# RMSNorm and matrix product on one core: the last four output tiles stored one by one, the very last in two pieces of 68 and 60 rows

## The chip, the cores and the metric

The kernel runs on one core of one Trainium2 chip. The time is the device time of one execution in microseconds (us). A core has engines that run side by side: TensorE (PE, with its weight loads shown apart as PEld), VectorE (DVE), ScalarE (ACT), GpSimd (POOL), and SyncE (SP), which here does nothing but issue DMA transfers and wait. Sixteen DMA engines carry the transfers between the chip's memory (HBM) and the core's own memory.

## The reference

```python
def reference(x, gamma, weight, eps):
    rms = np.sqrt(np.mean(x ** 2, axis=-1, keepdims=True) + eps)
    x_norm = x / rms * gamma
    return np.matmul(x_norm, weight).astype(np.float32)
```

x has 16 x 1024 = 16,384 rows of 512 numbers, weight is 512 x 768, and the output has 16,384 rows of 768 numbers, all float32. So 33.6 MB of x and 1.6 MB of weights are read, and 50.3 MB are written.

## The kernel before, in words

The rows are cut into 128 tiles of 128 rows. Each tile is brought in, cast to bfloat16 on GpSimd, turned by TensorE (four 128-column blocks, taken two at a time as 32-bit words), multiplied with the weights (already multiplied by gamma), and the product is scaled with the row's factor 1/rms on its way out of the accumulator: ScalarE does this for even tiles, VectorE for odd ones. The factor comes from squares summed on ScalarE.

Tiles are held in groups of eight: one output buffer `ot` holds 128 partitions x 8 tiles x 768 numbers, and there are three such buffers. In a group, partition p holds eight consecutive rows of the output, so that tile t of the group is row t of each partition's eight. A store of n tiles therefore writes, per partition, one run of n x 3,072 bytes; runs of neighbouring partitions lie eight rows apart.

`stretches` (line 46) says in which pieces a group is loaded or stored: as a rule all eight tiles at once (3 MB per store), in smaller pieces at the start, and at the end. Line 57 sets the pieces of the stores: 4 and 4 tiles in the last group but one (tiles 112 to 119), and 2, 2, 2, 1, 1 in the last (tiles 120 to 127). `store` (line 149) is called after every tile and issues a DMA from SP when the tile is the last of its piece.

All loads and stores are issued by SP in the order of the program. The order is written out by hand (`manual_schedule`). SP waits for the engines that filled the buffer, and for the DMA that used the same one of eight completion semaphores before. After the last store it waits for all transfers to land, and the kernel ends.

The last two tiles (lines 288 to 294) are finished differently: each in two parts of 512 and 256 columns, each part with its own accumulator, the first scaled by ScalarE and the second by VectorE; then the tile is stored.

Of the kernel before, what the change touches and what calls it, by code (L numbers as in the profile page):

```python
# [18 lines left out]
def kernel(  # L19
# [8 lines left out]
    nc = tc.nc  # L28
    P = 128

    x = x.flatten_outer_dims()
    out = out.flatten_outer_dims()
# [3 lines left out]
    NT = N // P  # L36
    NP = NT // 2
    G = 8
    NG = NT // G
# [6 lines left out]
    def stretches(parts):  # L46
        first, size, i = {}, {}, 0
        for g in range(NG):
            for n in parts.get(g, [G]):
                for t in range(i, i + n):  # L50
                    first[t], size[t] = i, n
                i += n
        return first, size

    opening = [1, 2, 1, 2, 2]
    x_first, x_size = stretches({0: opening, 1: [4, 4]})
    o_first, o_size = stretches({0: opening, NG - 2: [4, 4], NG - 1: [2, 2, 2, 1, 1]})

    def rows(ap, i, n):
        if i < G:  # L60
            return ap[i * P:(i + n) * P, :].rearrange("(p t) d -> p t d", t=n)
        return ap.rearrange("(g p t) d -> g p t d", p=P, t=G)[i // G, :, i % G:i % G + n, :]
# [11 lines left out]
    x_tiles, xb_tiles, tp_tiles, rstd_of, xT_tiles, o_tiles = {}, {}, {}, {}, {}, {}  # L74

    def held(tiles, i, n=1):
        return tiles[i // G][:, i % G:i % G + n, :]
# [66 lines left out]
    def out_tile(i):  # L144
        if i // G not in o_tiles:
            o_tiles[i // G] = outp.tile([P, G, O], F32, name="ot")
        return o_tiles[i // G][:, i % G, :]

    def store(i):
        first, n = o_first[i], o_size[i]  # L150
        if i == first + n - 1:
            nc.sync.dma_start(out=rows(out, first, n), in_=held(o_tiles, first, n))

    def matmul(i, k, acc, lo, hi):
        nc.tensor.matmul(out=acc[:, lo:hi], lhsT=xT_tiles[i // 2][:, i % 2, k // 2, :, k % 2], rhs=w_bf[:, k, lo:hi],  # L155
# [10 lines left out]
    def finish_tile(i, acc, engine):  # L166
        scale(engine, out_tile(i), acc[:, :O], rstd_of[i])
        store(i)
# [16 lines left out]
    with tc.manual_schedule():  # L185
# [102 lines left out]
        for i in (NT - 2, NT - 1):  # L288
            for lo, hi, engine in ((0, WIDE, nc.scalar), (WIDE, O, nc.vector)):
                a = accumulator()  # L290
                for k in range(K):
                    matmul(i, k, a, lo, hi)
                scale(engine, out_tile(i)[:, lo:hi], a[:, lo:hi], rstd_of[i])
            store(i)
# [35 lines left out]
```

## Time and profile before

| what | us |
|---|---|
| median of 9 runs | 211.26 |
| lowest and highest of them | 210.8, 212.88 |
| the profiled execution, its own time | 211.27 |
| its span (first to last instruction) | 209.5 |
| TensorE busy | 198.4 |
| ScalarE busy | 158.2 |
| VectorE busy | 111.7 |
| GpSimd busy | 66.3 |

In the profile, a busy row is a string of digits, one for each fortieth of the span (5.2 us): 9 means busy for 90% or more. The DMA row is the mean busy share of the sixteen DMA engines, and GB/s is what they moved. In a table of stretches each row has the window, its length, the busy time and number of instructions of PE, PEld, DVE, ACT and POOL, and then the granted TensorE clock, the DMA share and GB/s. A row of waits names who waited, at which line, for whom: total us, number, longest.

The stores as the page lists them, with size and median time from issue to landing:

```profile
out_dram<-ot SPq DMA_DIRECT2D x13, 3072.0 KB, 20.3
...
out_dram<-ot SPq DMA_DIRECT2D x6, 768.0 KB, 7.3
out_dram<-ot SPq DMA_DIRECT2D x2, 1536.0 KB, 9.3
...
out_dram<-ot SPq DMA_DIRECT2D x4, 384.0 KB, 18.0
```

The four stores of 384 KB are two at the start of the kernel and the two of tiles 126 and 127. At the end of the kernel SP issues stores at these times, in us from the start of the span: tiles 120-121 at 195.26, 122-123 at 198.68, 124-125 at 200.73, tile 126 at 201.49, tile 127 at 202.79.

### The profile page before, as it was taken

How to read it: one execution, taken by the hardware profiler on the slowest of the kernel's cores; microseconds unless marked ns; L12 is line 12 of the kernel's file. 1: busy time of each engine (PE TensorE's matmuls, PEld its weight loads, DVE VectorE, ACT ScalarE, POOL GpSimd, SP SyncE). 2: the span in 40 equal slices, each digit the busy share in tenths (PEclk: the TensorE clock that was granted, in tenths of full speed). 3: DMA queues.
4: the chain of work that ended last, by engine and by line, in shares of the span. 5: the costliest groups of instructions: out<-in, count | busy, mean ns of one | idle time of the engine just before them, and what ended most of it. 6: DMA issues, size and time to landing. Idle time of an engine off the chain costs nothing.

```text
span 209.5 us, 3555 instructions
## 1 busy us (share of the span) xinstructions
PE 198.4 (95%) x1268; PEld 137.5 (66%) x1293; DVE 111.7 (53%) x204; ACT 158.2 (76%) x388; POOL 66.3 (32%) x71
## 2 busy tenths in 40 slices
PE   7799999999999999999999999999999999999960
PEld 3466766677666676667766667666776666766630
DVE  2565565466456545644654565456446545654630
ACT  4699778778777877887787778778877877787830
POOL 1256543233323323332332233233323323310000
PEclk9999999999999999999999999999999999999996
DMA  6999999999999999999999999999999999998992
GB/s 225 410 426 441 382 403 427 419 443 424 443 419 418 447 418 433 422 421 444 416 444 416 443 424 427 436 415 438 421 433 419 436 432 430 422 415 369 381 369 110
DMA packets 7206, 85.69 MB, mean 409 GB/s; under 512 B 1042, under 2 KB 1044, under 8 KB 3220
## 3 DMA queue, kind: packets, MB, share of 16 engines
q1 hardware_dynamic: 6912, 85.46, 96.8%
q8 instruction: 10, 0.16, 0.3%
q10 hardware_dynamic: 276, 0.00, 0.1%
q14 instruction: 8, 0.07, 0.1%
HBM read 35.13 MB, written 50.33 MB: 408 GB/s over the span
## 4 chain that ended last, share of the span: by engine, by line
PE 93%; DVE 2%; issue 1%; ACT 1%
PE ops L155 78%; PE tp L120 13%; PE ops L210 1%; DVE ot L139 1%; DVE xT L127 1%; ACT ot L137 0%; DVE xb L93 0%; ACT jk L97 0%; DVE w_bf L139 0%; PE tp L224 0%; ACT rms L101 0%; DVE warm L201 0%; DVE rstd L103 0%; DVE eps_sb L203 0%
## 5 line engine op out<-in xcount | busy, mean ns | idle before, releaser
L155 PE MATMUL ops<-w_bf,xT 128*128 128x512 bf16 (+1 forms) x999 | 192.5, 324 | 1.9 <-DVE w_bf L139 0.6
L155 PEld LDWEIGHTS <-xT 128*128 128x128 bf16 x1024 | 100.2, 98 | 57.0 <-issue 1.0
L93 POOL CAST xb<-xt 128x1024 bf16<-128x1024 f32 (+1 forms) x65 | 65.6, 1014 | 118.7 <-PE tp L120 103.8
L127 DVE COPY xT<-tp 128x1024 bf16<-128x1024 bf16 (+1 forms) x67 | 44.5, 666 | 80.9 <-PE tp L120 80.9
L137 ACT ACTIVATE ot<-ops,rstd 128x768 f32<-128x768 f32 (+1 forms) x65 | 58.1, 894 | 37.8 <-PE ops L155 36.9
L97 ACT ACTIVATE jk<-xt 128x512 bf16<-128x512 f32 x128 | 78.7, 619 | 1.3 <-DMA xt<-in_x_dram 1.3
L120 PE MATMUL tp<-ident_f,xb 128*128 128x128 f32 x256 | 69.0, 274 | 0.7 <-DVE xb L93 0.6
L139 DVE TENSOR_SCALAR ot<-ops,rstd 128x768 f32<-128x768 f32 (+1 forms) x65 | 64.5, 992 | 2.9 <-PE ops L155 2.8
L120 PEld LDWEIGHTS tp<-ident_f,xb 128*128 128x128 f32 x256 | 35.9, 141 | 4.1 <-issue 1.1
L97 ACT ACTIVATION_READ_ACCUMULATOR jk<-xt 128x1 f32 x128 | 24.4, 191 | 0.0
L101 ACT ACTIVATE rms<-ssq,eps_sb 128x2 f32<-128x2 f32 (+1 forms) x64 | 18.9, 296 | 2.0
L103 DVE RECIPROCAL rstd<-rms 128x2 f32<-128x2 f32 (+1 forms) x64 | 9.9, 155 | 3.2 <-ACT rms L101 3.1
L210 PE MATMUL ops<-warm 128*128 128x512 bf16 x11 | 4.2, 523 | 1.2 <-DVE eps_sb L203 1.2
L210 PEld LDWEIGHTS <-warm 128*128 128x128 bf16 x11 | 1.3, 129 | 2.5 <-DVE eps_sb L203 1.2
L137 ACT ACTIVATE w_bf<-w_f,g_sb 128x768 bf16<-128x768 f32 x2 | 1.9, 936 | 1.4 <-DMA w_f<-in_weight_dram 1.4
L192 ACT ACT_TABLE_LOAD x1 | 1.3, 1283 | 1.7 <-issue 1.7
L93 DVE CAST xb<-xt 128x512 bf16<-128x512 f32 x2 | 1.2, 592 | 2.4 <-DMA xt<-in_x_dram 2.4
L139 DVE TENSOR_SCALAR w_bf<-w_f,g_sb 128x512 bf16<-128x512 f32 (+2 forms) x3 | 1.4, 481 | 0.5 <-DMA w_f<-in_weight_dram 0.5
L224 PEld LDWEIGHTS tp<-ident_f,g_row 2*128 2x128 f32 x2 | 0.3, 201 | 0.8 <-issue 0.8
L201 DVE MEMSET warm<- 128x256 uint32 x1 | 0.3, 272 | 0.9 <-PEq L311 0.9
L224 PE MATMUL tp<-ident_f,g_row 2*128 2x2 f32 x2 | 0.4, 265 | 0.0
L226 DVE COPY g_sb<-tp 128x4 f32<-128x4 f32 x1 | 0.2, 163 | 0.4 <-PE tp L224 0.4
(7 smaller groups left out, 1.0 us busy)
## 6 DMA issues: line engine op xcount, KB each, us to landing
out_dram<-ot SPq DMA_DIRECT2D x13, 3072.0 KB, 20.3
xt<-in_x_dram SPq DMA_DIRECT2D x14, 2048.0 KB, 24.8
out_dram<-ot SPq DMA_DIRECT2D x6, 768.0 KB, 7.3
out_dram<-ot SPq DMA_DIRECT2D x2, 1536.0 KB, 9.3
xt<-in_x_dram SPq DMA_DIRECT2D x2, 1024.0 KB, 11.2
xt<-in_x_dram SPq DMA_DIRECT2D x3, 512.0 KB, 5.8
w_f<-in_weight_dram SPq DMA_DIRECT2D x2, 768.0 KB, 6.1
out_dram<-ot SPq DMA_DIRECT2D x4, 384.0 KB, 18.0
```

The source lines that it names most:

```text
L93: engine.tensor_copy(out=xb_tiles[i // 2][:, i % 2:i % 2 + n, :], in_=held(x_tiles, i, n))
L97: nc.scalar.activation(out=jk, in_=held(x_tiles, i)[:, 0, :], func=AF.Square, accum_out=ssq)
L101: nc.scalar.activation(out=rms[:, :n], in_=ssq[:, :n], func=AF.Sqrt, scale=1.0 / D, bias=eps_sb)
L103: nc.vector.reciprocal(out=rstd[:, :n], in_=rms[:, :n])
L120: nc.tensor.transpose(out=tp_tiles[j][:, t, h, :], in_=words[:, lo:lo + P], identity=ident_f)
L127: nc.vector.tensor_copy(out=dst[:, t:t + n, :], in_=src[:, t:t + n, :])
L137: nc.scalar.mul(out=dst, in_=src, mul=r)
L139: nc.vector.tensor_single_scalar(out=dst, in_=src, scalar=r, op=mybir.AluOpType.mult)
L155: nc.tensor.matmul(out=acc[:, lo:hi], lhsT=xT_tiles[i // 2][:, i % 2, k // 2, :, k % 2], rhs=w_bf[:, k, lo:hi], start=(k == 0), stop=(k == ...
L192: nc.scalar.preload_act_table(AF.Sqrt)
L210: nc.tensor.matmul(out=spare[:, :WIDE], lhsT=warm[:, :P], rhs=warm, start=True, stop=True)
L224: nc.tensor.transpose(out=gp[:, c, :], in_=g_row[:, :, c], identity=ident_f[:2, :2])
```

## The change

The last group is stored in pieces of 2, 2, 1, 1, 1 and 1 tiles, so tiles 124 and 125 go apart. The store of tile 127 is issued as two DMAs: first its partitions 60 to 127 (68 rows), then its partitions 0 to 59 (60 rows). Nothing that is computed changes. On SP's queue there are two more DMAs; the instructions of the other engines stay in the same order.

```diff
-    o_first, o_size = stretches({0: opening, NG - 2: [4, 4], NG - 1: [2, 2, 2, 1, 1]})
+    o_first, o_size = stretches({0: opening, NG - 2: [4, 4], NG - 1: [2, 2, 1, 1, 1, 1]})
...
     def store(i):
         first, n = o_first[i], o_size[i]
         if i == first + n - 1:
-            nc.sync.dma_start(out=rows(out, first, n), in_=held(o_tiles, first, n))
+            for lo, hi in ((60, P), (0, 60)) if i == NT - 1 else ((0, P),):
+                nc.sync.dma_start(out=rows(out, first, n)[lo:hi], in_=held(o_tiles, first, n)[lo:hi])
```

## The prediction, before the changed kernel was run

> **What bounds the kernel now.** I read the page first, then what SP (the engine that issues the DMAs) waits for, then the stretches of the last 20 us, then the trace's records of single DMA packets and of the semaphore steps at their landing.
>
> ```profile
> span 209.5 us, 3555 instructions
> PE 198.4 (95%) x1268; PEld 137.5 (66%) x1293; DVE 111.7 (53%) x204; ACT 158.2 (76%) x388; POOL 66.3 (32%) x71
> ...
> DMA  6999999999999999999999999999999999998992
> GB/s 225 410 426 441 382 403 427 419 443 424 443 419 418 447 418 433 422 421 444 416 444 416 443 424 427 436 415 438 421 433 419 436 432 430 422 415 369 381 369 110
> ```
>
> Two resources are full up to slice 39: TensorE and the sixteen DMA engines. The chain of waits gives TensorE 93%, but the change touches no matmul; what it touches begins where TensorE stops.
>
> ```profile
> 201.80 0.69 ACT L137 ACTIVATE ot<-ops,rstd 128x512 f32<-128x512 f32 x1 [0.61 <-PE ops L155]
> 201.82 0.38 PE L155 MATMUL ops<-w_bf,xT 128*128 128x256 bf16 x2
> 202.24 0.48 DVE L139 TENSOR_SCALAR ot<-ops,rstd 128x256 f32<-128x256 f32 x1 [0.82 <-PE ops L155]
> 202.79 0.33 SPq L152 DMA_DIRECT2D out_dram<-ot  x1
> ```
>
> The last arithmetic ends at 202.72 and the last store is issued at 202.79. The span ends 6.7 us later.
>
> ```profile
> SPq L325 <- DMA out_dram<-ot: 5.3, 1, 5.3
> ```
>
> SP's last real wait is 5.3 us for stores to land (203.23 to 208.54); 0.9 us of closing instructions follow. So what sets the end is the last DMA landing. How full are the engines in that wait?
>
> ```profile
> 190.00:195.00 5.00, 5.00 (x36) 3.52 (x34) 3.12 (x5) 4.28 (x12) 0.00 (x0) 1.00 0.86 360
> 195.00:199.00 4.00, 3.95 (x26) 2.53 (x25) 1.95 (x5) 3.08 (x7) 0.00 (x0) 1.00 0.92 381
> 199.00:202.00 3.00, 3.00 (x20) 1.76 (x18) 1.50 (x2) 1.12 (x3) 0.00 (x0) 1.00 0.84 345
> 202.00:204.00 2.00, 0.20 (x2) 0.00 (x0) 0.48 (x1) 0.49 (x1) 0.00 (x0) 1.00 0.99 399
> 204.00:205.00 1.00, 0.00 (x0) 0.00 (x0) 0.00 (x0) 0.00 (x0) 0.00 (x0) 1.00 1.01 409
> 205.00:206.00 1.00, 0.00 (x0) 0.00 (x0) 0.00 (x0) 0.00 (x0) 0.00 (x0) 1.00 0.53 206
> 206.00:207.00 1.00, 0.00 (x0) 0.00 (x0) 0.00 (x0) 0.00 (x0) 0.00 (x0) 0.60 0.09 37
> 207.00:208.50 1.50, 0.00 (x0) 0.00 (x0) 0.00 (x0) 0.00 (x0) 0.00 (x0) 0.50 0.04 16
> ```
>
> The DMA share (last column but one) is the finding. All sixteen are busy to 205; then it falls to 0.09 (about 1.5 engines of 16), then 0.04 over 1.5 us, which is one engine for 1 us. **One engine ends the kernel alone.** The landing records say by how much: each store raises its semaphore once per engine. Times in us:
>
> | store | most engines (median) | second last | last |
> |---|---|---|---|
> | tiles 122-123 | 201.84 | 203.15 | 204.78 |
> | tiles 124-125 | 203.92 | 205.01 | 206.63 |
> | tile 126 | 204.87 | 205.92 | 207.56 |
> | tile 127 | 205.87 | 206.86 | 208.48 |
>
> Following packets that abut, the last engine has no gap from 193 us on and lies 2.6 us behind the others; a second lies 1.0 behind. The last one's backlog is old: in the 3 MB stores its packets of 24,576 bytes take 941 to 964 ns where other engines take 912. In this tail its 3,072-byte packets start every 0.118 us as the others' do. Eight of them, its eight rows of tile 127, are the step from 207.56 to 208.48.
>
> **The change part by part.**
>
> *Tiles 124 and 125 stored apart.* One DMA of 6,144-byte packets becomes two of 3,072. Removed: nothing from the total of bytes. Added: one issue of 0.33 us on SP and one 4-byte semaphore packet of 9 ns per engine. Tile 124 is ready at 199.24 (ScalarE's 198.34 + 0.90), so it is issued at about 199.3 while SP would otherwise sleep until 200.73; tile 125 keeps its issue time. Gain on the ordinary engines: they finish 122-123 at 201.44 and start 124-125 at 201.59, so at most 0.15 us of idle. Gain on the last engine: **nothing**, it has no gap to fill; it pays the 9 ns.
>
> *Tile 127 as 68 and 60 rows.* Which engine gets which row decides everything. The packet records carry no engine number. The Trainium skill, "DMA: Bandwidth & Descriptors", section "Why a DMA increments its semaphore by 16 and not by 1", says that such a DMA uses the largest number up to 16 that divides its outer size, and the lowest-numbered engines. This trace agrees as far as it goes (the two-row gamma load made exactly two 1,024-byte packets). By it, 68 rows go as 17 each to engines 0 to 3 and 60 rows as 4 each to 0 to 14. So engines 0-3 have 21 rows instead of 8, engines 4-14 have 4, engine 15 has none. With 0.118 us per row, from the landing of tile 126:
>
> - ordinary engine among 0-3: 204.87 - 0.15 + 21 x 0.118 = 207.20
> - second-last engine among 4-14: 205.92 + 0.47 = 206.39
> - last engine, if it is 15: 207.56, done with tile 126
>
> The end moves from 208.48 to 207.56: **-0.92 us**. Only 0.36 us lower lies the load on engines 0-3, so nothing more is to be had. That those four run alone costs no speed, I take it: the one engine alone at the end kept 0.118 (bounds: 0 to +0.4 us, a fifth on 2 us, of which 0.36 is hidden).
>
> *SP's queue.* The second half is issued 0.38 us after the first (0.33 and its step), at 203.17; nothing is behind it but the closing waits. Its semaphore and the first half's are reused ones whose earlier stores landed by 192.75 and 196.57, so no new wait. From issue to first packet on an idle engine took 0.86 us (200.73 to 201.59), so the second half can start at 204.0, before engines 4-14 have finished tile 126. Hidden. If the closing waits see it land last instead, one more step of 0.06.
>
> *A rule that speaks against it.* The row first: in the tail, on an engine with a backlog, the last data packet of tile 126, its 9 ns semaphore packet and the first packet of tile 127 follow without a gap, and landing trails the last packet by about 0.4 us, beside the next packets. The same page ("Rules for kernel authors") says not to split a transfer into partition halves, since they serialize, and ("Anatomy of one DMA") gives each DMA some 2.0 us fixed plus bytes at 436 GB/s. By that, the pieces of 209 and 184 KB cost 2.48 + 2.42 = 4.9 us in turn against 2.9 whole: +2.0 us, 213.3. By the rows a further DMA in a full queue costs 0.01 us. I take the rows: the page's fixed part is mostly the wait for the receipt, which overlaps here.
>
> **Sum.** Span 209.48 - 0.92 = 208.56. The profiled execution took 211.27 (1.79 outside the span), so 210.35; the median before, 211.26, is the same within 0.01. I say **210.3 us**, -0.45%. A measurement of this kernel tells about 0.5% (1.06 us, to 210.2 or 212.3) from no change, so this is just inside "same".
>
> **Rivals.** All hang on which engine is last, and the trace can't number it.
>
> 1. *The last engine is one of 4-14.* It keeps 4 rows: 207.56 + 0.47 = 208.03, -0.45: **210.8**. For: the same page ("Latency and other measured facts") calls engines 7 and 15 usually the slower ones, and this trace does show exactly one with slow packets. Against: 15 is the other candidate, and the page blames a cause of DMAs issued from GpSimd, which this kernel has none of.
> 2. *The second-last engine is one of 0-3.* It would have 205.92 + 2.48 = 208.40, -0.08: **211.2**, nothing gained. For: it lags 1.0 us, enough to fill the slack; instruction fetches of 16 KB that take about 1 us each fall on single engines, so it can be any. Against: 4 of 15 by chance.
> 3. *The last engine is one of 0-3.* Then it gets 13 rows more: 207.56 + 21 x 0.118 = 210.04, +1.56: **212.8**, slower. It decides as soon as an engine of 0-3 lands tile 126 after 206.0 (208.48 - 2.48). For: nothing in the records excludes it, and 4 of 16 by chance. Against: the pace of this engine is its own, all through the run, and the page names two engines outside 0-3.
> 4. *The rows don't split as stated* (68 rows on sixteen engines, say): nothing moves, 211.2.
>
> **Numbers.** The forecast 0.58; rival 1 0.14; 2 0.13; 3 with the fixed-cost case 0.11; 4 0.04. Around the forecast I allow 0.35 us each way: the slow pace may add 0.05 to the eight rows, engines 0-3 may lose up to 0.4, the median of a set of runs moves by 0.2. Range 209.9 to 211.5 holds the forecast, 1, 2 and 4, and leaves rival 3 out. Faster by over 0.5%: half of the forecast's share (its centre is 0.15 from the bound) and a little of rival 1, 0.33. Slower 0.12. Within 0.5%: 0.55.
>
> **What would show it.** The DMA share of the last 1.5 us before the end: about four engines (0.25) and not one. SP's wait for the stores shorter by the 0.38 of the extra issue and by 0.92. Tile 124's issue near 199.3. In the landings: the 68-row store steps its semaphore by data four times, near 206.7; the last landing of all belongs to tile 126 at 207.56. Wrong if the last landing is a 68-row one after 208, or if the last engine still carries rows of tile 127.

## The result: slower by about one microsecond

The changed kernel took 212.14 us (median of 16 runs, 211.69 to 214.68); the kernel before, run beside it, 211.15 us (53 runs). The ratio is 1.0056, with a 95% interval of 1.004 to 1.0072. The forecast was 210.3 us, with a range of 209.9 to 211.5.

The profiled execution of the changed kernel took 213.24 us, 1.1 more than its median, so two differences have to be kept apart. First the head of the page, then the row of the costliest group in the page before and after: TensorE's matmuls, with busy time and mean ns, and after the second bar the idle time before them and what ended it. (Line 155 of the kernel before is line 158 of the changed one.)

```profile
span 211.5 us, 3558 instructions
PE 198.4 (94%) x1268; PEld 137.4 (65%) x1293; DVE 111.6 (53%) x204; ACT 158.2 (75%) x388; POOL 66.3 (31%) x71
```

```profile
L155 PE MATMUL ops<-w_bf,xT 128*128 128x512 bf16 (+1 forms) x999 | 192.5, 324 | 1.9 <-DVE w_bf L139 0.6
```

```profile
L158 PE MATMUL ops<-w_bf,xT 128*128 128x512 bf16 (+1 forms) x999 | 192.5, 324 | 3.3 <-DVE w_bf L139 2.0
```

In this execution the weights came later at the very start (TensorE waited 2.0 us for them and not 0.6), and all that follows is 1.2 us later: the last arithmetic ends at 203.92 (before: 202.72). The change touches nothing there, and the first experiment's kernel, which lacks the half of the change that costs, shows such a start too (1.7 us). What the change does is seen from 203.92 on. The stretches of the changed kernel, with the DMA share in the last column but one:

```profile
204.00:205.00 1.00, 0.00 (x0) 0.00 (x0) 0.00 (x0) 0.00 (x0) 0.00 (x0) 1.00 1.01 399
205.00:206.00 1.00, 0.00 (x0) 0.00 (x0) 0.00 (x0) 0.00 (x0) 0.00 (x0) 1.00 0.98 326
206.00:207.00 1.00, 0.00 (x0) 0.00 (x0) 0.00 (x0) 0.00 (x0) 0.00 (x0) 0.57 0.65 123
207.00:208.00 1.00, 0.00 (x0) 0.00 (x0) 0.00 (x0) 0.00 (x0) 0.00 (x0) 0.50 0.25 61
208.00:209.00 1.00, 0.00 (x0) 0.00 (x0) 0.00 (x0) 0.00 (x0) 0.00 (x0) 0.50 0.24 92
209.00:210.00 1.00, 0.00 (x0) 0.00 (x0) 0.00 (x0) 0.00 (x0) 0.00 (x0) 0.50 0.12 49
```

Where the kernel before had one engine at work for the last two microseconds (share 0.04 to 0.09), there are now four (0.25). And they are slow: at 207 to 208 a share of 0.25 moves 61 GB/s, at 208 to 209 nearly the same share moves 92. Before, all sixteen moved 409 at a share of 1.01, which is 102 for a quarter. So the four engines are busy, but their packets take longer. The packet records say the same: of the 512 packets of 3,072 bytes of the last four tiles, 39 take over 0.18 us (up to 0.94), between 205.48 and 208.03. The longest such packet in the tail of the kernel before takes 0.136. Below, "slow packets" are those over 0.18 us, and their excess is the time that each takes over 0.121 us, summed; in the changed kernel it is 9.3 us.

The landings (us; each store raises its semaphore once per engine):

| store, changed kernel | most engines (median) | last |
|---|---|---|
| tile 125 | 205.01 | 206.37 |
| tile 126 | 206.02 | 207.31 |
| tile 127, 68 rows, four engines | 209.14, 209.29, 209.30 | 209.88 |
| tile 127, 60 rows, eleven other engines | 206.79 | 207.77 |
| tile 127, 60 rows, the same four engines | 209.62, 209.76, 209.77 | 210.36 |

The last landing is now that of an engine of the four, 6.44 us after the last arithmetic; before it was 208.48 - 202.72 = 5.76. That is 0.68 us later. SP's wait for the stores reads 5.3 us in both profiles (it now begins 0.6 later, after the issues of both pieces), which alone tells nothing:

```profile
SPq L328 <- DMA out_dram<-ot: 5.3, 1, 5.3
```

### The profile page after: what moved, and what is told of

Same layout as the page of the kernel before. It is cut to its first block, busy times and chain, and to the rows that moved or that the text cites. A ratio compares the mean times of both kernels' runs of the same rounds, so it can differ in the third digit from the quotient of the medians.

```text
span 211.5 us, 3558 instructions
## 1 busy us (share of the span) xinstructions
PE 198.4 (94%) x1268; PEld 137.4 (65%) x1293; DVE 111.6 (53%) x204; ACT 158.2 (75%) x388; POOL 66.3 (31%) x71
## 4 chain that ended last, share of the span: by engine, by line
PE 90%; DMA 3%; DVE 1%; ACT 1%; issue 1%; SPq 0%; DVEq 0%
PE ops L158 77%; PE tp L120 13%; DMA w_f<-in_weight_dram 3%; DVE ot L139 1%; ACT ot L137 0%; SPq L82 0%; ACT jk L97 0%; DVE w_bf L139 0%; DVE xT L127 0%; ACT rms L101 0%; DVE rstd L103 0%; DVEq L139 0%
```

## The experiments

Where no ratio is given, the time is that of a single run.

**1. Which half costs.** Three kernels: the first half of the change alone, the second alone, and another way to spare engine 15.

The first half alone:

```diff
-            for lo, hi in ((60, P), (0, 60)) if i == NT - 1 else ((0, P),):
+            for lo, hi in ((0, P),) if i == NT - 1 else ((0, P),):
```

> Tiles 124 and 125 stored apart, tile 127 whole: the first half of the change alone. Slow-packet theory (the 68 and 60 rows make the DMA engines' packets slow, which costs some 1.3 us in the changed kernel's trace): this half costs nothing, the last store's 3,072-byte packets stay near 0.12 us, time 211.0 to 211.2, ratio 0.999 to 1.000. Rival (the extra issue and the split of 124-125 is what costs): ratio 1.004 or more.

Measured: 211.27 us against 211.11, ratio 1.0001 (0.9993 to 1.0009), and not one packet over 0.18 us. A further DMA and the pieces of one tile cost nothing.

The second half alone:

```diff
-    o_first, o_size = stretches({0: opening, NG - 2: [4, 4], NG - 1: [2, 2, 1, 1, 1, 1]})
+    o_first, o_size = stretches({0: opening, NG - 2: [4, 4], NG - 1: [2, 2, 2, 1, 1]})
```

> Tile 127 as 68 and 60 rows, tiles 124-125 stored together: the second half alone. Slow-packet theory: about the whole loss, +0.9 us, ratio 1.004 to 1.007, and packets of 0.3 to 0.9 us in the last 4 us. Rival (pieces): ratio 1.000.

Measured: 212.36 us, ratio 1.0053 (1.0032 to 1.0073), 32 packets over 0.18 us. The whole loss is in the 68 and 60 rows.

The kernel with the first half alone shows one thing more. In its profiled execution the last arithmetic ended at 205.45, 2.7 us later than before and later than in the changed kernel. Yet its span is 209.9, only 0.4 longer than before. Its stretches:

```profile
206.00:207.00 1.00, 0.00 (x0) 0.00 (x0) 0.00 (x0) 0.00 (x0) 0.00 (x0) 1.00 1.00 396
207.00:208.00 1.00, 0.00 (x0) 0.00 (x0) 0.00 (x0) 0.00 (x0) 0.00 (x0) 0.64 0.99 396
208.00:209.00 1.00, 0.00 (x0) 0.00 (x0) 0.00 (x0) 0.00 (x0) 0.00 (x0) 0.50 0.11 40
```

All sixteen engines end nearly together; the one with the old backlog lands 0.34 us behind the median (208.82 and 208.48). That it caught up while the others waited for the late arithmetic is an inference from this one profile. With the tile stored whole, two things can set the end: the engine with the backlog, at 208.5 to 208.8 in these two executions, and the ordinary engines, some 3.1 us after the last arithmetic. The first hides arithmetic that is up to 2.6 us late (5.76 less some 3.1). The other traces agree: in the twelve kernels that issue tile 126 whole before the arithmetic ends, its last landing lies between 207.16 and 208.29, while the arithmetic ends anywhere between 202.43 and 205.45; the one with the latest arithmetic has 207.90. The stretches of the second kernel (68 and 60 rows), whose arithmetic ended at 202.66, show the other case:

```profile
205.00:206.00 1.00, 0.00 (x0) 0.00 (x0) 0.00 (x0) 0.00 (x0) 0.00 (x0) 0.95 0.60 114
206.00:207.00 1.00, 0.00 (x0) 0.00 (x0) 0.00 (x0) 0.00 (x0) 0.00 (x0) 0.50 0.37 117
207.00:208.00 1.00, 0.00 (x0) 0.00 (x0) 0.00 (x0) 0.00 (x0) 0.00 (x0) 0.50 0.25 101
208.00:209.00 1.00, 0.00 (x0) 0.00 (x0) 0.00 (x0) 0.00 (x0) 0.00 (x0) 0.50 0.07 28
```

| kernel | last arithmetic | last landing | difference | who is last |
|---|---|---|---|---|
| before | 202.72 | 208.48 | 5.76 | one engine with backlog |
| pieces only | 205.45 | 208.82 | 3.37 | the same, 0.34 behind the others |
| changed | 203.92 | 210.36 | 6.44 | the four engines |
| 68 and 60 only | 202.66 | 209.09 | 6.43 | the four engines |
| output rows moved (below) | 203.44 | 209.89 | 6.45 | the four engines |

With 68 and 60 rows in this order the end follows the arithmetic at 6.44 us in three executions, so arithmetic that comes late now moves the end.

120 and 8 rows:

```diff
-            for lo, hi in ((60, P), (0, 60)) if i == NT - 1 else ((0, P),):
+            for lo, hi in ((0, 120), (120, P)) if i == NT - 1 else ((0, P),):
```

> Tile 127 as 120 rows (15 engines, 8 rows each) and 8 rows (8 engines, one each). If the engine that ends last is number 15, it has no row of tile 127 and the end moves up by 0.9 us, to 210.2 or so (ratio 0.996). If it is 8 to 14 nothing moves (1.000), if 0 to 7 it ends 0.12 us later (1.0005). Slow-packet theory adds: the 15 engines no longer read the rows that they read in a 128-row store, so packets of 0.2 to 0.9 us appear and the time grows by 0.5 to 1.5 us (ratio 1.002 to 1.007) whichever engine is last. Rival (only the 21 rows on four engines are slow): packets stay at 0.12.

Measured: 211.29 us, ratio 1.0001 (0.9985 to 1.0017). The last engine landed tile 126 at 208.02, its share of the 120 rows at 208.94 and one of the 8 rows at 209.12: it has a share of each, so it is not number 15, and by the row of eight it is one of 0 to 7. There were 40 packets over 0.18 us, on engines that had two microseconds to spare; they cost nothing.

**2. Which engine is last.**

```diff
+            for lo, hi in ((0, 112), (112, 119), (119, 127), (127, P)) if i == NT - 1 else ((0, P),):
```

> Tile 127 as 112, 7, 8 and 1 rows: 7 rows for each of 16 engines, then one for engines 0 to 6, one for 0 to 7, one for 0. The number of row packets that the last engine carries after tile 126 tells which it is: 7 for 8 to 15, 8 for number 7, 9 or 10 for 0 to 6. In the changed kernel's trace the last engine took 4 of the 60 rows after tile 126, so it is one of 4 to 14: I expect 8 packets (engine 7) or 7. If it is 15 after all: 7, and the 120-row run decides.

Measured: 211.71 us. After tile 126 (207.72) the last engine landed 7 rows at 208.52, one of the seven-row piece at 208.71, one of the eight-row piece at 208.90, but not the single row, so it is one of 1 to 6. In the changed kernel it took 4 of the 60 rows and none of the 68, so there it is one of 4 to 14. Together that leaves 4, 5 or 6, if it is always the same one.

```diff
+            for lo, hi in ((0, 112), (112, 117), (117, 123), (123, P)) if i == NT - 1 else ((0, P),):
```

> Tile 127 as 112, 5, 6 and 5 rows: one of the small pieces' rows each for engines 0 to 4, 0 to 5, 0 to 4. With the runs so far the last engine is 4, 5 or 6: after its 7 rows it carries 3 more if it is 4, 1 more if it is 5, none if it is 6 or more.

Measured: 212.32 us. The landings of the last engine: 209.02 with the 112 rows, then 209.20, 209.40 and 209.59, one for each small piece. **It is engine 4.** (The number 4 follows from the rule, taken over in the prediction, that a DMA uses the lowest-numbered engines; no record carries an engine's number. How many engines a piece uses is seen in the steps of its semaphore, and all pieces agree with the rule: four for 68 and 76 rows, fifteen for 60 and 120, thirteen for 52, and 8, 7, 6 and 5 for themselves.) It takes three traces read together: this one leaves 0 to 4, the one before it 1 to 6, the changed kernel's 4 to 14. Two traces further down agree: with 76 rows first, and with the 60 rows first, the last engine took four rows of the smaller piece and none of the larger. The second-last one carries none of the small pieces in either run, so it lies above 7.

**3. What makes the packets slow.** First without the 60 rows, which are left out of the output:

```diff
+            for lo, hi in ((60, P),) if i == NT - 1 else ((0, P),):
```

> Of tile 127 only rows 60 to 127 are stored (68 rows); the other 60 rows are left out of the output. If the four engines slow each other (two pairs of them read rows 34 partitions apart at the same time), packets over 0.18 us stay on the four engines, and their 17 rows take clearly more than 2.0 us. If it is the 60-row store beside them that makes them slow, nearly all packets are 0.12 us and the 17 rows take 2.0 us after the last row of tile 126.

Measured: 211.68 us, 17 packets over 0.18 us with 2.6 us of excess. From the median landing of tile 126 (205.81) the 17 rows took 2.63 to 3.01 us; in the changed kernel 3.12 to 3.86. So the 60-row store beside them is a part of it, not all. (The last landing, 208.82, is still that of a 68-row share.)

Two halves of 64 rows:

```diff
+            for lo, hi in ((0, 64), (64, P)) if i == NT - 1 else ((0, P),):
```

> Tile 127 as two halves of 64 rows, each on all sixteen engines with 4 rows. Theory (engines that do not keep to the partitions they read in a 128-row store meet at the same entry of the memory): many packets of 0.2 to 0.5 us, on engines that have 2 us of slack, so the time stays within 0.2 us of before. Rival (a DMA on fewer than sixteen engines is slow as such): no slow packet.

Measured: 211.33 us, 39 packets over 0.18 us, 5.5 us of excess, and no effect on the end: the last landing, 208.46, comes 5.82 us after the arithmetic and is that of the engine with the backlog. Here every DMA runs on sixteen engines, so "fewer engines" is not what makes a packet slow. Its stretch from 204 to 205 moves 310 GB/s at a full share:

```profile
204.00:205.00 1.00, 0.00 (x0) 0.00 (x0) 0.00 (x0) 0.00 (x0) 0.00 (x0) 1.00 1.08 310
```

76 and 52 rows:

```diff
+            for lo, hi in ((52, P), (0, 52)) if i == NT - 1 else ((0, P),):
```

> Tile 127 as 76 rows (19 on each of engines 0 to 3) and 52 rows (4 on each of thirteen engines). Four engines now carry 23 rows instead of 21, but rows read at the same time by two of them are 38 partitions apart instead of 34. If meeting at the same entry slows the four, the slow packets become fewer and the end comes no later than with 68 and 60 in spite of 8 more rows in all: ratio 1.000 to 1.004. If the loss is the number of rows alone, or the 60-row store beside, the end is later by 0.24 us or more: ratio 1.006 to 1.008.

Measured: 212.72 us, ratio 1.0077 (1.0059 to 1.0094), as the rival said. In its profile the slow packets are fewer (28, with 6.7 us; before this 32 and 39, with 8.3 and 9.3), and the last landing comes 6.27 us after the arithmetic, a little sooner than with 68 rows. The timed runs do not bear that out.

The 60 rows first:

```diff
+            for lo, hi in ((0, 60), (60, P)) if i == NT - 1 else ((0, P),):
```

> The changed kernel with the two pieces in the other order, 60 rows first. Engines 0 to 3 then read their 17 rows when most other engines are done. If it is the meeting with rows that other engines still read that makes the 17 rows slow, the slow packets lose most of their excess (9.3 us in all in the changed kernel) and the ratio falls to 1.000 to 1.003. If the four slow each other, or if the number of rows alone decides, it stays at 1.004 to 1.007.

Measured: 211.95 us, ratio 1.0053 (1.0035 to 1.0071), 40 packets over 0.18 us, 7.5 us of excess. The order is no remedy. In this one profile the engine with the backlog ended last (208.75), the four just before it (208.57).

The output rows of the last eight tiles at other places:

```diff
-        if i < G:
+        if i < G or ap is out and i >= NT - G:
```

> The changed kernel with the output rows of the last eight tiles at other places: neighbouring partitions write neighbouring rows (3 KB apart) instead of rows 24 KB apart, so the last 1,024 output rows are permuted. The reads from the core's memory stay as they are. If the slow packets come from the reading side, they stay: 25 to 45 packets over 0.18 us with 7 to 11 us of excess. If they come from where rows are written, their number changes by more than half.

Measured: 212.76 us, 37 packets over 0.18 us with 9.2 us, against 39 with 9.3. Moving the rows that are written did not change it.

The four engines with as little beside them as possible; tile 126 and the smaller piece of tile 127 are left out of the output:

```diff
-        if i == first + n - 1:
-            for lo, hi in ((60, P), (0, 60)) if i == NT - 1 else ((0, P),):
+        if i == first + n - 1 and i != NT - 2:
+            for lo, hi in ((60, P),) if i == NT - 1 else ((0, P),):
```

> Left out of the output: tile 126, and rows 0 to 59 of tile 127. The 68 rows of tile 127 then go to engines 0 to 3 when most engines have nothing left to read. If it is other engines' rows that they meet, the 17 rows of each take 2.0 us and hardly a packet is over 0.18 us. If the four meet each other (first with third, second with fourth, 34 partitions apart[...]), slow packets remain, in pairs, and the 17 rows take 2.3 to 3.0 us.

```diff
+            for lo, hi in ((52, P),) if i == NT - 1 else ((0, P),):
```

> Left out: tile 126, and rows 0 to 51 of tile 127. 76 rows, 19 on each of the four engines, 38 partitions apart for first and third. If the four meet each other when 34 apart, there are fewer slow packets than with 68 rows alone and the 19 rows take close to 2.24 us. If both runs show hardly a slow packet, the meeting with the other twelve engines' rows is what costs; if both show as many, distance has nothing to do with it.

Measured: 210.5 and 210.21 us. With 68 rows 12 packets over 0.18 us (2.1 us of excess), and from the first packet to the last the four took 2.6 to 3.0 us for 17 rows; with 76 rows 13 packets (2.0 us), 2.7 to 2.9 us for 19. Half a microsecond of delay or more remains on each engine with hardly anything beside. Distance makes little difference in the count; only the late slow packets (after 205.6) are missing with 76.

What follows: slow packets appear in every kernel that stores tile 127 otherwise than as one DMA of 128 rows (112, 120, twice 64, 68, 76 rows), and in neither of the two that do not. They are not a matter of the distance between the written rows (one other layout was tried), of the use of few engines as such, or of the other piece alone. The Trainium skill ("SBUF — State Buffer", section "Door 1: The DMA port swizzle") maps the 128 partitions to sixteen ports in an interleaved way, and in a 128-row store each engine keeps to one port; if each engine of a piece takes a block of consecutive rows, which no run here shows, engines would meet at a port in pieces. That would fit the list. But by the same map and the same assumption no two of the four meet with 76 rows when they read in step, and 13 slow packets remained in the run with 76 rows alone. Since moving the written rows did nothing, the reading side or the way in which the transfers reach the engines is the likelier place; **which of them stays open**, and neither was tested by itself.

**4. A version meant to gain.** If engine 4 is last, it can be spared a row here and there:

```diff
-    o_first, o_size = stretches({0: opening, NG - 2: [4, 4], NG - 1: [2, 2, 1, 1, 1, 1]})
+    o_first, o_size = stretches({0: opening, NG - 2: [4, 4], NG - 1: [2, 2, 2, 1, 1]})
...
+            for lo, hi in ((0, 112), (112, 116), (116, 120), (120, 124), (124, P)) if i in (NT - 3, NT - 1) else ((0, P),):
```

> Pieces of 2, 2, 2, 1, 1 tiles; tiles 124-125 and tile 127 each stored as 112 rows (7 per engine) and four times 4 rows (one each on engines 0 to 3). If engine 4 ends last, as the runs so far say, it is spared one row of 6 KB and one of 3 KB: 0.23 + 0.12 = 0.35 us, and engines 0 to 3 get 3 rows more of each, 1.05 us, inside their slack of 2.6. Ratio 0.998 to 0.999. If SP's nine further issues (0.38 us each) or slow packets give it back: 1.000 to 1.004.

Measured: 212.43 us, ratio 1.0071 (1.0043 to 1.0098). The four-row pieces of tiles 124 and 125 took SP 0.39 to 0.93 us each to issue, not the 0.33 of a whole store, and so the store of tile 126 was issued at 203.95, 1.1 us after the arithmetic had ended (202.84); before it went out at 201.49, while tile 127 was still being computed. There were also 42 slow packets, and the last landing (209.59) is that of an engine with a row of every four-row piece, one of 0 to 3, which landed its part of the 112 rows at 208.90. So the work moved to engines 0 to 3 set the end again. No kernel tried here that writes the whole output beats the one before.

## Why the prediction was wrong

Both signs that the prediction named for being wrong are there: 68-row landings after 208 (209.14 to 209.88), and rows of tile 127 on the engine with the backlog (four, landed at 207.77).

- *What bounds the end* was right for the kernel before: one engine with an old backlog, 2.6 us behind the others.
- *Tiles 124 and 125 apart: nothing.* Right (1.0001), and with it the choice of the rows against the rule of a fixed 2.0 us for each DMA.
- *The last engine is 15.* This step failed. It is engine 4, which is rival 1's case: it kept 4 rows of tile 127 (206.37 for tile 125, 207.31 for tile 126, 207.77 for tile 127 in the changed kernel) and could gain 0.47 us, not 0.92. The Trainium skill's "DMA: Bandwidth & Descriptors", section "Latency and other measured facts", names 7 and 15 as the usually slower ones; the runs here decide against both for the engine that lags in this kernel. By this step alone the forecast would still have been a small gain, 210.8.
- *That those four run alone costs no speed (bounds 0 to +0.4 us, of which 0.36 is hidden).* This step failed too, and it turned the sign. The sum gave an engine of 0 to 3 a landing at 207.20, 4.48 us after the arithmetic. In the three kernels with 68 rows first, three of the four land 5.6 to 5.9 us after it, the slowest 6.4: 1.1 to 2.0 us more than worked out, of which the slow packets of the 17 rows are 1.1 to 1.9 (3.1 to 3.9 us against 2.0). I had taken the pace from the engine that ends alone. Its packets were near in time and equal in size, but they belonged to a store of 128 rows, and the 17 rows did not; that is the difference that the experiments show, whatever lies behind it.
- *The rival on the slower side* had the right bearers, engines 0 to 3, but for the wrong reason. It needed one of them to come with a backlog and land tile 126 late. In the changed kernel all engines but the one with the backlog landed tile 126 within 0.3 us of the median (206.30 at the latest, against 206.02); it was the rows after it that took longer. Its size, +1.56, was too large.
- *The fixed-cost case* (+2.0 us) was not it: a further DMA alone cost nothing (1.0001), two halves of 64 rows took 211.33 us against 211.00, and the landings of the pieces overlap. The section that I took it from gives the fixed 2.0 us for DMAs issued from GpSimd, and the stores here go out from SP.
- What I had not seen is the second meaning of the backlog: it is a cover. Before, arithmetic that ends up to 2.6 us late hardly moves the end. The change put a path of 6.44 us behind the arithmetic, and that cover is gone. By 6.44 - 5.76 and the 0.10 that the closing waits took more, the loss is 0.78 us at the arithmetic of the profile before; the median lost 0.99. That late starts make up the rest is in keeping with the wide spread of the changed kernel (211.69 to 214.68) beside that of the pieces alone (210.76 to 211.8), and with the kernel with the 60 rows first, whose eleven runs fall into two groups 0.8 us apart (211.5 to 211.95 and 212.74 to 213.24). It was not measured by itself, and whether the changed program starts late more often than the one before is not known.

## What to carry to other kernels

When one engine ends late, find out which it is before shifting work away from it: here two runs with stores of 8, 7, 6 or 5 rows, read from the landings together with those of the changed kernel, named it. Do not take the pace of rows that are given to other engines from whole 128-row stores. And slack behind a bound is not free to spend: it may be what hides late starts, so an edit that fills it makes the time follow them.

## What the runs showed of the hardware that I had not expected

- Packets of 3,072 bytes that take 0.121 us in 128-row stores took up to 0.95 us, over a stretch of one to three microseconds, in each kernel that stored the last tile cut by rows, even in halves on all sixteen engines. From 12 to 42 packets were over 0.18 us. Cut by tiles, each with 128 rows, they kept 0.12.
- The DMA engine that lags is number 4 of 0 to 15, if it is the same one in the three traces that together name it and engines are counted by the rule above. In the profiles one engine lagged by 1.3 to 3.7 us behind the median in the landings of tile 126, and by 0.4 where the arithmetic ended at 205.45.
- The start is not steady: the last arithmetic ended between 202.43 and 205.45 in the fifteen profiled executions, and in the two profiles with whole tiles the time hardly showed it (211.27 us at 202.72, 211.67 at 205.45).
